# Moving the SBUF tiles of a two-layer encoder trunk to other start addresses

## The chip, the cores and the metric

The kernel runs on one core of a Trainium2 chip. The metric is device time in microseconds (us) of one execution. Engines are named as the profile names them: PE multiplies, PEld is PE's loading of the stationary operand, DVE (VectorE) and ACT (ScalarE) work element by element, SP issues the DMAs. All addresses below are bytes within one SBUF partition.

## The reference, cut to what matters

The input is 256 tokens of 1024 features. Two layers, each: half a SwiGLU step, a mixer step, half a SwiGLU step; every step is normalised, scaled and shifted by values that a condition vector `c` gives, and added back through a gate. Layer 0 mixes by pooling, layer 1 by differential attention. All in float32.

```python
for i in range(DEPTH):
    mod = (c_act @ mod_w[i] + mod_b[i])[:, None, :]
    sh0, sc0, g0, sh1, sc1, g1, sh2, sc2, g2 = jnp.split(mod, N_MOD, axis=-1)
    h = modulate(rms_norm(x, norm_g[i, 0]), sh0, sc0)
    x = x + 0.5 * g0 * swiglu(h, ffn_w_gu[i, 0], ffn_w_down[i, 0])
    h = modulate(rms_norm(x, norm_g[i, 1]), sh1, sc1)
    ...  # y: pool_mixer (i = 0) or diff_attention (i = 1)
    x = x + g1 * y
    h = modulate(rms_norm(x, norm_g[i, 2]), sh2, sc2)
    x = x + 0.5 * g2 * swiglu(h, ffn_w_gu[i, 1], ffn_w_down[i, 1])
return rms_norm(x, final_g)
```

## The kernel before, in words

Activations stay in SBUF, features on partitions, 256 tokens along the row. The weights come from HBM once, as 312 units of up to 128 x 1024 float32 (4096 bytes a row), in the order in which they are used. To keep float32 accuracy with the narrower matmul type fp32r, every operand is held as two parts. `split_unit` (lines 304 to 316) loads a unit into `raw`, lets ACT write `hi` (line 313) and DVE write `lo = raw - hi` (line 314). These live in three rings: `raw` with 5 buffers, `hi` and `lo` with 6 each. The activations have parts too: `hh`/`hl` (the normalised input), `ahl` (the inner activations; `ah`, `al` are its halves), `xh`/`xl` (the not yet normalised input).

A product of two split operands is three matmuls (`prod3`, lines 331 to 335): L333 multiplies the two high parts, L334 and L335 a high by a low part. In most of the program a 128 x 128 piece of the weights, from `hi` or `lo`, is the stationary operand (512 bytes of each partition's row are loaded) and 256 tokens of `hh`, `hl`, `ah` or `al` are the moving operand (1024 bytes of each row). In `v_unit` and in the pooling mixer it is the other way round: `hi` or `lo` moves and a piece of the activations is loaded. The first weights of a step use `xh`/`xl` instead (`mm_deferred`, L431 to L433), with the normalisation applied afterwards; there a moving row of `xh` is 258 columns wide, and the rows of `xh` lie 258 x 4 = 1032 bytes apart.

Beside this, DVE does the products of the condition vector with `mod_w` (line 272, one tile `u` of 128 x 1024 at a time, spread over the program as a background).

A scheduling layer places the instructions and inserts the waits. Where a tile lies is decided by the order in which the pools are opened and by the sizes of the tiles in them, each rounded up to 32 bytes. Before, small tiles stood among large ones: `eps1` (4 bytes, 32 with rounding) ahead of `xT`, the rows of `xh` with 8 odd bytes each, and `vecT`, `mod0`, `b1` and the other vectors between `cact` and the weights' rings.

Of the kernel before, what the change touches and what calls it, by code (L numbers as in the profile page):

```python
# [11 lines left out]
F32 = mybir.dt.float32  # L12
F32R = mybir.dt.float32r
# [3 lines left out]
AX = mybir.AxisListType  # L17

P = 128
D = 1024  # L20
KD = D // P
T = 256
NT = T // P
DFF = 2816
KF = DFF // P
EPS = 1e-6
# [36 lines left out]
def weight_units():  # L63

    def block(name, lead, r0, r1, c0, c1):
        return name, (*lead, slice(r0, r1), slice(c0, c1))

    def halves(name, lead, c0):
        yield block(name, lead, 0, 512, c0, c0 + UW)
        yield block(name, lead, 512, 1024, c0, c0 + UW)  # L70

    def ffn(i, s):
        first = 0
        if (i, s) == (0, 0):
            first = EARLY
            for k in range(KD):
                for n in range(2):
                    yield block("ffn_w_gu", (i, s), k * P, (k + 1) * P, n * DFF, n * DFF + EARLY * UW)
        for j in range(first, KF // 2):
            for n in range(2):  # L80
                yield from halves("ffn_w_gu", (i, s), n * DFF + j * UW)
        for dp in range(D // UW):
            for k0, k1 in DOWN_K:
                yield block("ffn_w_down", (i, s), k0 * P, k1 * P, dp * UW, (dp + 1) * UW)

# [5 lines left out]
    for tok in SCHED.split():  # L91
        n, u = tok[0], int(tok[1])
        if n in "qkv":
            yield from halves("diff_w_qkv", (), "qkv".index(n) * D + u * UW)
        elif n in "AB":
# [5 lines left out]
def unit_shape(ix):  # L101

    return (ix[-2].stop - ix[-2].start) // P, ix[-1].stop - ix[-1].start

# [8 lines left out]
def lay_out(inputs):  # L113
# [4 lines left out]
    head = np.concatenate([np.arange(16, 64), np.arange(0, 16), np.arange(64, P)])  # L118
    order = np.concatenate([h * P + head for h in range(2 * HEADS)] + [np.arange(2 * D, 3 * D)])
    w["diff_w_qkv"] = w["diff_w_qkv"][:, order]  # L120
    w["pool_w"] = w["pool_w"].reshape(D, UW)
    w["k_pool"] = consts["k_pool"]
# [20 lines left out]
def trunk(ctx: ExitStack, tc: tile.TileContext, x, c, mod_w, small, weights, diff_lambda, k_rope, out):  # L143
    nc = tc.nc
    V, S, PE = nc.vector, nc.scalar, nc.tensor

    cpool = ctx.enter_context(tc.tile_pool(name="cpool", bufs=1))
    rawp = ctx.enter_context(tc.tile_pool(name="rawp", bufs=RAW_BUFS))
    hip = ctx.enter_context(tc.tile_pool(name="hip", bufs=SPLIT_BUFS))
    lop = ctx.enter_context(tc.tile_pool(name="lop", bufs=SPLIT_BUFS))  # L150
    tmp = ctx.enter_context(tc.tile_pool(name="tmp", bufs=2))
    ps = ctx.enter_context(tc.tile_pool(name="ps", bufs=4, space=bass.MemoryType.PSUM))

    uid = [0]

    def nm(s):
        uid[0] += 1
        return f"{s}_{uid[0]}"

    def const(shape, name, dt=F32):  # L160
        return cpool.tile(shape, dt, tag=name, name=name)

    def psum():
        return ps.tile([P, 512], F32, tag="mm", name=nm("mm"), bufs=4)
# [4 lines left out]
    def psmall():  # L169
        return ps.tile([P, 512], F32, tag="st", name=nm("st"), bufs=2)  # L170
# [2 lines left out]
        return tmp.tile([P, n], F32, tag=tag, name=nm(tag), bufs=bufs)  # L173

    def tiny(n, dt=F32, tag="tiny", bufs=8):
        return tmp.tile([P, n], dt, tag=tag, name=nm(tag), bufs=bufs)

    def tinyw(n, dt=F32):
        return tiny(n, dt, "tinyw", 8)

    def tinyv(n, dt=F32):
        return tiny(n, dt, "tinyv", 6)
# [4 lines left out]
        return v.rearrange("p (k o) -> p k o", o=1)  # L187


    ident = const([P, P], "ident")  # L190
    make_identity(nc, ident)
    ones = const([P, P], "ones")
    V.memset(ones, 1.0)

    pt = psum()
    for _ in range(WARM):
        PE.matmul(pt[:, :P], ones, ones, start=True, stop=True)

    eps1 = const([P, 1], "eps1")
    V.memset(eps1, 1.0)  # L200

    xT = const([P, KD, T], "xT")
    xh = const([P, KD, T + 2], "xh", F32R)
    xl = const([P, KD, T], "xl", F32R)
    hh = const([P, KD, T], "hh", F32R)
    hl = const([P, KD, T], "hl", F32R)
# [3 lines left out]
    def warm(f, after):  # L210

        S.activation(tiny(1, tag="warm", bufs=1), after, f, scale=0.0, bias=eps1)


    cact = const([P, D], "cact")
    for half in range(2):
# [132 lines left out]
    def newton(y, y0, v, t):  # L349
        V.tensor_tensor(t, y0, y0, ALU.mult)  # L350
        V.scalar_tensor_tensor(t, t, -0.5, v, ALU.mult, ALU.mult)
        V.scalar_tensor_tensor(y, t, 1.5, y0, ALU.add, ALU.mult)
# [27 lines left out]
    def rstd_cols():  # L380

        pt = psmall()
        for q in range(NT):
            PE.matmul(pt[:, q:q + 1], acc[:, q * P:(q + 1) * P], ones[:, 0:1], start=True, stop=True)
        v = tiny(NT)
        V.tensor_scalar(v, pt[:, :NT], 1.0 / D, EPS, ALU.mult, ALU.add)
        y = tmp.tile([P, NT], F32, tag="rstdc", name=nm("rstdc"), bufs=2)
        y0 = tiny(NT)
        S.activation(y0, v, AF.Abs_reciprocal_sqrt)
        newton(y, y0, v, tiny(NT))  # L390
        return y
# [167 lines left out]
    def pool_mixer(nxt):  # L559
# [5 lines left out]
        S.activation(hh[:, :, 0:P], bb, AF.Copy)  # L565
        V.tensor_tensor(hl[:, :, 0:P], bb, hh[:, :, 0:P].bitcast(F32), ALU.subtract)
        rstd = rstd_cols()

        def group(pt, g, q, lh, ll):
# [358 lines left out]
```

## Time and profile before

| | us |
|---|---|
| median of 3 runs | 934.19 |
| lowest and highest of them | 933.71, 940.46 |
| the profiled execution | 942.75 |
| its span, first to last instruction | 940.9 |
| PE busy in the span | 911.2 (97%) |
| DVE busy | 743.6 (79%) |
| ACT busy | 505.4 (54%) |

The profiled execution is 8.6 us above the median. Matmuls overlap: each is shown as about 280 ns long, while the next one starts some 118 ns after it. What a matmul costs PE in a row of matmuls is therefore the distance from one start to the next, and not its own length; the timeline gives the starts to 10 ns, so that the distance is taken over many matmuls.

### The profile page before, as it was taken

The numbers are of one execution on the slowest core, as the hardware profiler recorded it, in microseconds if no ns is written. First come the engines' busy times: TensorE is split into PE (matmuls) and PEld (weight loads), VectorE is DVE, ScalarE is ACT, GpSimd is POOL, SyncE is SP. The second block draws the span as 40 slices with busy tenths as digits, with TensorE's granted clock in tenths as the row PEclk, the third lists the DMA queues.
The fourth block names the chain that finished last, engine by engine and source line by source line (L and its number), as shares of the span: only waits on it lengthen the run. The fifth ranks groups of instructions, "written<-read, shape, count | busy, mean of one in ns | idle before, by whom it ended". The sixth has DMA issues, their size and how long they took to land.

```text
span 940.9 us, 18753 instructions
## 1 busy us (share of the span) xinstructions
PE 911.2 (97%) x7532; PEld 897.5 (95%) x7532; DVE 743.6 (79%) x1211; ACT 505.4 (54%) x771; POOL 0.7 (0%) x6
## 2 busy tenths in 40 slices
PE   7899999899999999999999999999999999999997
PEld 7898889798999999999999999999999999999996
DVE  5868888789999777887988888888888897666451
ACT  5564435445665445455654454557777765444541
POOL 0000000000000000000000000000000000000000
PEclk9999999999999999999999999999999999999998
DMA  8988999888659887898599888855546548655531
GB/s 339 355 301 304 317 335 357 298 313 285 245 192 324 288 282 265 299 317 285 179 356 324 311 304 306 264 194 162 158 132 224 185 154 277 193 182 181 169 122 45
DMA packets 68727, 238.18 MB, mean 253 GB/s; under 512 B 7968, under 2 KB 9248, under 8 KB 68640
## 3 DMA queue, kind: packets, MB, share of 16 engines
q1 hardware_dynamic: 68496, 236.88, 73.8%
q8 instruction: 59, 0.97, 0.4%
q14 instruction: 28, 0.23, 0.1%
q10 hardware_dynamic: 144, 0.11, 0.0%
HBM read 234.86 MB, written 1.05 MB: 251 GB/s over the span
## 4 chain that ended last, share of the span: by engine, by line
PE 72%; DMA 12%; DVE 8%; ACT 4%; issue 3%; SPq 1%; DVEq 0%; ACTq 0%
PE mm L333 18%; PE mm L335 18%; PE mm L334 17%; DMA raw<-in_weights_dram 10%; DVE u L272 3%; DVE lo L314 3%; PE hd L335 3%; PE hd L333 3%; PE hd L334 3%; ACT hi L313 2%; PE mm L431 2%; PE mm L433 2%; PE mm L432 2%; PE hd L644 1%; DMA u<-in_mod_w_dram 1%
## 5 line engine op out<-in xcount | busy, mean ns | idle before, releaser
L313 ACT ACTIVATE hi<-raw 128x1024 fp32r<-128x1024 f32 (+1 forms) x312 | 318.6, 1025 | 339.2 <-PE mm L334 170.0
L314 DVE TENSOR_TENSOR lo<-raw,hi 128x1024 fp32r<-128x1024 f32 (+1 forms) x312 | 366.6, 1181 | 139.7 <-ACT hi L313 137.5
L335 PE MATMUL mm<-hh,lo 128*128 128x256 f32 x992 | 276.6, 281 | 4.4 <-DVE lo L314 4.4
L333 PE MATMUL mm<-hh,hi 128*128 128x256 f32 x992 | 277.7, 281 | 0.1
L334 PE MATMUL mm<-hl,hi 128*128 128x256 f32 x992 | 276.7, 280 | 0.0
L335 PE MATMUL mm<-ahl,lo 128*128 128x256 f32 x768 | 215.1, 280 | 2.2 <-DVE lo L314 2.2
L333 PE MATMUL mm<-ahl,hi 128*128 128x256 f32 x768 | 215.1, 280 | 1.8 <-ACT hi L313 1.8
L334 PE MATMUL mm<-ahl,hi 128*128 128x256 f32 x768 | 214.7, 280 | 0.0
L335 PEld LDWEIGHTS mm<-hh,lo 128*128 128x128 f32 x992 | 185.5, 188 | 6.6 <-DVE lo L314 6.0
L333 PEld LDWEIGHTS mm<-hh,hi 128*128 128x128 f32 x992 | 186.6, 188 | 1.3 <-ACT hh L420 0.4
L334 PEld LDWEIGHTS mm<-hl,hi 128*128 128x128 f32 x992 | 186.6, 188 | 0.0
L272 DVE SCALAR_TENSOR_TENSOR u<-u,cact 128x1024 f32<-128x1024 f32 x144 | 173.9, 1218 | 0.2 <-DMA u<-in_mod_w_dram 0.2
L335 PEld LDWEIGHTS mm<-ahl,lo 128*128 128x128 f32 x768 | 144.1, 188 | 3.4 <-DVE lo L314 3.4
L333 PEld LDWEIGHTS mm<-ahl,hi 128*128 128x128 f32 x768 | 144.2, 188 | 2.5 <-ACT hi L313 2.2
L334 PEld LDWEIGHTS mm<-ahl,hi 128*128 128x128 f32 x768 | 144.2, 188 | 0.0
L333 PE MATMUL hd<-hh,hi 128*128 128x256 f32 x288 | 81.2, 282 | 5.9 <-ACT hi L313 5.9
L335 PE MATMUL hd<-hh,lo 128*128 128x256 f32 x288 | 81.6, 283 | 3.9 <-DVE lo L314 3.9
L334 PE MATMUL hd<-hl,hi 128*128 128x256 f32 x288 | 80.7, 280 | 0.0
L333 PEld LDWEIGHTS hd<-hh,hi 128*128 128x128 f32 x288 | 54.3, 189 | 6.5 <-ACT hi L313 6.5
L335 PEld LDWEIGHTS hd<-hh,lo 128*128 128x128 f32 x288 | 54.3, 188 | 5.2 <-DVE lo L314 5.1
L432 PE MATMUL mm<-xl,hi 128*128 128x256 f32 x208 | 58.8, 285 | 0.0
L433 PE MATMUL mm<-xh,lo 128*128 128x258 f32 x208 | 58.3, 282 | 0.0
(199 smaller groups left out, 1034.7 us busy)
## 6 DMA issues: line engine op xcount, KB each, us to landing
raw<-in_weights_dram SPq DMA_DIRECT2D x264, 512.0 KB, 4.6
u<-in_mod_w_dram SPq DMA_DIRECT2D x144, 512.0 KB, 5.5
raw<-in_weights_dram SPq DMA_DIRECT2D x48, 384.0 KB, 5.0
xT<-in_x_dram SPq DMA_DIRECT2D x2, 512.0 KB, 5.0
out_dram<-u SPq DMA_DIRECT2D x4, 256.0 KB, 2.5
cact<-in_c_dram SPq DMA_DIRECT2D x1, 512.0 KB, 7.1
pk<-qk SPq DMA_DIRECT2D x16, 32.0 KB, 2.9
qk<-pk SPq DMA_DIRECT2D x16, 32.0 KB, 2.0
```

Source lines behind the costliest of these rows:

```text
L272: return V.scalar_tensor_tensor(raw, raw, 1.0, cact, ALU.mult, ALU.mult, accum_out=out)
L313: S.activation(hi[:, :w], raw[:, :w], AF.Copy)
L314: splits.append(V.tensor_tensor(lo[:, :w], raw[:, :w], hi[:, :w].bitcast(F32), ALU.subtract).ins)
L333: PE.matmul(o, lh, rh, start=start, stop=False, **kw)
L334: PE.matmul(o, lh, rl, start=False, stop=False, **kw)
L335: PE.matmul(o, ll, rh, start=False, stop=stop, **kw)
L431: PE.matmul(o[:, :T + 2], hi[:, kk, cs], xh[:, k, :], start=(k == 0), stop=False)
L432: PE.matmul(o[:, :T], hi[:, kk, cs], xl[:, k, :], start=False, stop=False)
L433: PE.matmul(o[:, :T + 2], lo[:, kk, cs], xh[:, k, :], start=False, stop=(k == KD - 1))
L644: PE.matmul(sc[c2][:, q * T:(q + 1) * T], l[pr, 0, qs], r[pr, 1, :], start=(n == 0), stop=(n == 2))
```

## The change

The change moves tiles in SBUF. Tiles whose row is not a multiple of 16 elements (64 bytes), and the small temporaries, go into a pool of their own behind everything else; the row of `xh` is widened to 272 columns, of which 258 are used; and one 64-byte tile `gap`, which is written once and never read, stands between the activations and the rings.

```diff
@@
 P = 128
+LINE = 16
@@
     cpool = ctx.enter_context(tc.tile_pool(name="cpool", bufs=1))
+    gap = ctx.enter_context(tc.tile_pool(name="gap", bufs=1))
     rawp = ctx.enter_context(tc.tile_pool(name="rawp", bufs=RAW_BUFS))
...
     tmp = ctx.enter_context(tc.tile_pool(name="tmp", bufs=2))
+    small_p = ctx.enter_context(tc.tile_pool(name="small_p", bufs=1))
@@
     def const(shape, name, dt=F32):
-        return cpool.tile(shape, dt, tag=name, name=name)
+        return (cpool if shape[-1] % LINE == 0 else small_p).tile(shape, dt, tag=name, name=name)
@@
     def tiny(n, dt=F32, tag="tiny", bufs=8):
-        return tmp.tile([P, n], dt, tag=tag, name=nm(tag), bufs=bufs)
+        return small_p.tile([P, n], dt, tag=tag, name=nm(tag), bufs=bufs)
@@
+    V.memset(gap.tile([P, LINE], F32, tag="gap", name="gap"), 0.0)
@@
-    xh = const([P, KD, T + 2], "xh", F32R)
+    xh = const([P, KD, T + LINE], "xh", F32R)[:, :, :T + 2]
@@
-        y = tmp.tile([P, NT], F32, tag="rstdc", name=nm("rstdc"), bufs=2)
+        y = tiny(NT, F32, "rstdc", 2)
```

On PE, ACT, SP and GpSimd the instructions, their order and their waits are the same in both programs; on DVE one MEMSET of 128 x 16 (`gap`) is added as the first instruction. All else that differs is the start addresses. Counted off from the sizes and the order of the tiles, they are (start of the row, modulo 256 and modulo 64):

```
tile                            before: mod 256, mod 64     after: mod 256, mod 64
xT                              160, 32                     128, 0
xh (row of each k)              160 + 8k, 32 + 8k           128 + 64k, 0
xl, hh, hl, ahl, cact           224, 32                     128, 0
raw, hi, lo (all buffers)       160, 32                     192, 0
u, t, qk, o, pk                 192, 0                      192, 0
ident, ones                     128, 0                      128, 0
acc                             128, 0                      128, 0
rstd, rope                      0, 0                        192, 0
```

All further steps inside a tile (from one k or one buffer to the next, from one 128-column piece to the next) are multiples of 512 bytes, so every matmul that reads a tile other than `xh` starts on the residue shown. The weights' parts start 64 bytes below the activations' residue before (160 against 224), and 64 bytes above it after (192 against 128).

## Rows read from the trace of the kernel before

**Rows 1.** The page: the span, each engine's busy time (share of the span, x instructions), and the chain of work that ended last, shared out by engine.
```profile
span 940.9 us, 18753 instructions
PE 911.2 (97%) x7532; PEld 897.5 (95%) x7532; DVE 743.6 (79%) x1211; ACT 505.4 (54%) x771; POOL 0.7 (0%) x6
...
PE 72%; DMA 12%; DVE 8%; ACT 4%; issue 3%; SPq 1%; DVEq 0%; ACTq 0%
```

**Rows 2.** Busy time in stretches of the program: from:to in us, then length, PE, PEld, DVE, ACT, POOL busy us (x instructions), granted TensorE clock (1.00 is its upper level, 2.4 GHz), share of the DMA engines, GB/s. 182 to 239 is the end of the first feed-forward step and the start of the pooling mixer; 239, 437 and 737 begin stretches with `xh`/`xl`; 625 to 737 is the attention.
```profile
47.00:182.00 135.00, 124.13 (x1008) 119.74 (x1009) 110.36 (x156) 65.15 (x81) 0.00 (x0) 1.00 0.90 319
182.00:239.00 57.00, 54.47 (x436) 54.07 (x435) 49.53 (x80) 27.68 (x40) 0.00 (x0) 0.94 0.83 289
239.00:279.00 40.00, 39.42 (x327) 38.86 (x327) 39.33 (x86) 28.19 (x50) 0.00 (x0) 1.00 0.70 243
279.00:437.00 158.00, 158.00 (x1343) 158.00 (x1343) 126.21 (x171) 76.70 (x96) 0.00 (x0) 1.00 0.87 294
437.00:469.00 32.00, 31.99 (x265) 31.52 (x264) 29.70 (x64) 20.07 (x32) 0.00 (x0) 1.00 0.59 184
469.00:625.00 156.00, 156.00 (x1326) 156.00 (x1326) 130.43 (x183) 78.19 (x98) 0.00 (x0) 1.00 0.87 301
625.00:737.00 112.00, 111.11 (x912) 106.00 (x911) 95.93 (x233) 82.42 (x199) 0.00 (x0) 1.00 0.56 175
737.00:774.00 37.00, 36.91 (x305) 36.41 (x304) 35.28 (x77) 27.37 (x47) 0.00 (x0) 1.00 0.47 153
774.00:924.00 150.00, 150.00 (x1276) 149.97 (x1274) 89.94 (x103) 69.65 (x85) 0.00 (x0) 1.00 0.56 180
```

**Rows 3.** Who waited for whom from 47 to 182 us: waiting engine and line, what it waited for: us in total, times, longest us.
```profile
ACT hi L313 <- DMA raw<-in_weights_dram: 40.3, 25, 5.0
...
PEld mm L335 <- DVE lo L314: 8.9, 13, 1.2
```

**Rows 4.** The same view from 279 to 437 us.
```profile
ACT hi L313 <- PE mm L334: 50.3, 34, 2.2
...
ACT hi L313 <- DMA raw<-in_weights_dram: 2.8, 1, 2.8
```

**Rows 5.** Timeline of PE (start us, length us), first and last of 102 matmuls without a gap in the second feed-forward step of layer 0.
```profile
299.91 0.28 PE L335 MATMUL mm<-hh,lo 128*128 128x256 f32 x1
...
311.81 0.28 PE L334 MATMUL hd<-hl,hi 128*128 128x256 f32 x1
```

**Rows 6.** The same view, first and last of 47 matmuls in the first feed-forward step.
```profile
144.02 0.28 PE L333 MATMUL hd<-hh,hi 128*128 128x256 f32 x1
...
149.24 0.28 PE L334 MATMUL mm<-hl,hi 128*128 128x256 f32 x1
```

**Rows 7.** The same view, two runs in which the weights' parts move (`v_unit`): first and last of 48 matmuls, then first and last of 31.
```profile
674.43 0.28 PE L333 MATMUL mm<-hi,hh 128*128 128x256 f32 x1
...
679.96 0.28 PE L335 MATMUL mm<-hi,hl 128*128 128x256 f32 x1
...
700.80 0.28 PE L335 MATMUL mm<-hi,hl 128*128 128x256 f32 x1
...
704.20 0.28 PE L335 MATMUL mm<-hi,hl 128*128 128x256 f32 x1
```

**Rows 8.** The same view, runs of alike matmuls merged (first start, time to the end of the last, xcount): eight transposes of 128 columns (moving `ident`, loaded `u`), and sixteen products of attention weights with values (moving operand two pieces of 512 bytes of `ahl`, loaded operand `ahl` too).
```profile
704.32 1.04 PE L675 MATMUL st<-ident,u 128*128 128x128 f32 x8
...
723.39 2.07 PE L694 MATMUL st<-ahl 128*128 128x256 f32 x16
```

**Rows 9.** The same view, the three matmuls of `mm_deferred` on k = 4 (the one row of `xh` that starts on a multiple of 64 before) and the first on k = 5.
```profile
269.47 0.28 PE L431 MATMUL hd<-xh,hi 128*128 128x258 f32 x1
...
269.83 0.28 PE L431 MATMUL hd<-xh,hi 128*128 128x258 f32 x1
```

**Rows 10.** Groups of DVE and ACT instructions by shape (line, engine, operation, out<-in, shapes, xcount | busy us, mean ns of one | idle before).
```profile
L314 DVE TENSOR_TENSOR lo<-raw,hi 128x1024 fp32r<-128x1024 f32 x264 | 321.2, 1222 | 131.8 <-ACT hi L313 129.9
L272 DVE SCALAR_TENSOR_TENSOR u<-u,cact 128x1024 f32<-128x1024 f32 x144 | 173.9, 1218 | 0.2 <-DMA u<-in_mod_w_dram 0.2
...
L822 DVE TENSOR_TENSOR qk<-xT,pk 128x1024 f32<-128x1024 f32 x1 | 1.2, 1218 | 0.0
```

**Rows 11.** The page's DMA issues (KB each, median us from issue to landing).
```profile
raw<-in_weights_dram SPq DMA_DIRECT2D x264, 512.0 KB, 4.6
u<-in_mod_w_dram SPq DMA_DIRECT2D x144, 512.0 KB, 5.5
```

**Rows 12.** Timeline of DVE from the span's start.
```profile
0.83 0.17 DVE L193 MEMSET ones<- 128x128 f32 x1 [0.83 <-PEq L916]
0.95 0.06 DVE L200 MEMSET eps<- 128x1 f32 x1
```

**Rows 13.** The chain that ended last, in order of time, near its start.
```profile
2.96 7.94 DMA u<-in_mod_w_dram
```

## The prediction, on record before the result

> **What bounds the kernel now.** I read the page first. PE is busy 97% of the span and carries 72% of the chain that ended last; DMA carries 12% of it [rows 1]. Whether a cheaper matmul shortens the program is a question of the stretch, so the table by stage comes next [rows 2]. Up to 182 us the weights' supply sets the pace: PE is busy 124.1 of 135 us, the DMA engines 90%, and ACT's split waits 40.3 us for arriving weights, after which PE waits for `lo` [rows 2, 3]. From 279 on it is the other way round. PE has no idle time in 279 to 437, 469 to 625 and 774 to 924, and the split waits for PE to give a ring buffer back (50.3 us against 2.8 for DMA) [rows 2, 4]. There the time is the number of matmuls times the distance from one start to the next, and nothing else.
>
> That distance is the number to look at. In the long stretches it is 11.90 us over 101 steps, 117.8 ns [rows 5]. With the same tiles on the same residues, another run goes at 5.22 us over 46 steps, 113.5 ns [rows 6]. Where the weights' parts move and lie 64 bytes below the loaded operand, which for the moving operand is the relation that the change gives to all matmuls, one run has 5.53 over 47, 117.7 ns, and another 3.40 over 30, 113.3 ns [rows 7]. So there are two levels, 4.4 ns apart, held for a whole run, at a granted clock of 1.00 (2.4 GHz) throughout. Neither is set by the shape alone. Eight transposes, whose moving operand starts at 128 and whose loaded operand at 192 modulo 256 (the residues after the change), take 1.04 us; with 0.27 for the last that is 0.77 over 7, 110 ns [rows 8]. They move 128 columns and not 256, so they do not prove what 256 will do, but 113.4 less one more step of 4.4 is 109, and the two agree within the timeline's rounding.
>
> **The change part by part.** No instruction but one moves, so everything hangs on what an instruction takes at its new addresses.
>
> (a) *Moving and loaded operands on multiples of 64, weights 64 above.* The rows of before have no 256-column matmul at these residues. Its spacing is bounded from below by the transposes and the step of the levels (109), from above by a level higher than today's, 117.8 + 4.4 = 122.2. Nothing excludes a loss: sixteen products whose moving and loaded operands start on the same residue go at (2.07 - 0.28) / 15 = 119 ns [rows 8]. I take 109: the transposes have the addresses, and the run of 113.5 shows that 117.8 is no floor.
>
> The gain is then 8.8 ns for each matmul in a stretch that PE bounds:
> - 279 to 437, 469 to 625, 774 to 924: 1343 + 1326 + 1276 = 3945 matmuls, 34.7 us, all on the path.
> - The three stretches with `xh`/`xl` hold 327 + 265 + 305 = 897 matmuls, 7.9 us if all got it. Here DVE is busy 39.3 of 40, 29.7 of 32 and 35.3 of 37 us, so it binds right after PE, and rows of 258 columns need not reach the level of 256. I take half, 4.0.
> - Attention, 912 matmuls, 8.0 us if all got it; part are of other shapes, PE runs in short pieces and idles 0.9 us. I take a third, 2.7.
> - 182 to 239, 436 matmuls, 3.8 us if all got it. The DMA engines are 83% busy and PE idles 2.5 us; I take nothing, and nothing before 182, where PE would only wait longer.
> - After 924 some 60 matmuls, 0.5 us.
>
> Sum 41.9 us, with all counts from the table by stage [rows 2].
>
> [...] In rows 5 and 6 all starts are multiples of 32. [...]
>
> (b) *Rows of `xh` 1088 bytes apart.* On k = 4, the only row that starts on a multiple of 64 today, three matmuls take 0.36 us, 120 ns each [rows 9]: no better than the rest. Aligning `xh` alone, against weights that are not, buys nothing visible, which is why half was taken above.
>
> (c) *DVE and ACT at new addresses.* DVE takes 1222 ns for 1024 columns with `raw` and `hi` at 160, 1218 with `u` at 192 and `cact` at 224, 1218 with `xT` at 160: the start does not show [rows 10]. Zero, within 4 ns a unit, and 312 of those are 1.2 us on an engine that has 20% to spare.
>
> (d) *DMA into `raw` at 192 instead of 160.* A unit lands in 4.6 us at 160; `u` is at 192 already and takes 5.5 with the same bytes, by its place in the queue [rows 11]. I take zero; were it 1% of the supply before 182, it would be 1.4 us either way.
>
> (e) *The MEMSET of `gap`.* It stands ahead of `ones` on DVE; its kin take 0.06 and 0.17 us [rows 12]. PE's warm-up matmuls wait for them, but the first weights' work waits until about 10.9 us for `u` [rows 13], so that covers it. Uncovered it would be 0.17 us.
>
> *What is late next.* With 109 ns, 279 to 437 moves its bytes in 146 us and needs 294 x 117.8 / 109 = 318 GB/s, and 469 to 625 needs 325; the stretch in which supply binds has 319 [rows 2]. At worst the second one is held to 156 x 301 / 319 = 147.2 us instead of 144.3: 2.9 us of the gain. DVE's 130.4 us fit into 144. This goes into the range.
>
> The profiled execution is 942.75, so it would come out at 900.9; subtracted from the median of 934.19 the same 42 us give 892.
>
> **The rivals.**
> - *One level instead of two.* The matmuls go to 113.4, the level that before shows in short runs, and stay there: 4.4 / 8.8 of the sum, 21 us, 913. For it: this is the only better spacing that 256 columns show, and the weights-move runs, with the relation of the change, never fall under it. Against it: those runs still start 32 bytes off a multiple of 64.
> - *The change does not do what it is laid out for.* The level is picked by how a run starts (both levels occur on one set of residues), long runs settle on 117.8 again, and the time is 934, give or take 9. For it: the slow run with the moved weights has the new relation and 117.7 all the same; k = 4 of `xh` gains nothing. [...]
> - *Slower.* Two streams that start on whole lines 64 bytes apart meet each time, where streams half a line off miss each other, and matmuls settle one level higher, 122.2 ns. At 4.4 more for the matmuls of the sum that is 21 us, 955. It decides from 119.8 ns on, where the loss passes 1%. For it: the 119 ns of the products on one common residue. Against it: the transposes with these very residues are the quickest of all.
>
> **How the numbers follow.** Two levels down 0.50 (from 882, which is nearly the whole 8.8 ns everywhere, 54.9 us, to 904, if the spacing is 111.5), one level 0.20 (908 to 918), no change 0.18 (925 to 943), slower 0.12. A measurement of this kernel can tell about 1%, 9 us, from no change. The likeliest is 892. A range from 882 to 936 holds nearly all of the first case, the second, and some two thirds of the third, together about 0.8. Faster by over 1%: 0.50 + 0.20 = 0.70; within 1% 0.18; slower 0.12.
>
> **What would show it.** In the timeline after, starts in the long stretches 109 ns apart, and the 1343 matmuls of 279 to 437 done in 146 us. The spacing in `v_unit` and pooling, which get the relation that the main matmuls have today, will tell the 64 bytes from the alignment: if alignment alone is the cause they fall too, if the relation is, they go to 117.8. The start up to 182 us, DVE's 1222 ns and the units' landing time should stay. I am wrong if the spacing stays at 117.8 or rises, or if it falls and PE then waits for `lo` after 279.

## The result and the profile after

The changed kernel takes 927.93 us (median of 20 runs, 919.33 to 940.43), the kernel before, run beside it, 938.52 (20 runs, 932.89 to 944.51). The ratio is 0.987, 95% interval 0.9843 to 0.9896; the ratios here and below leave out a kernel's runs over 1.5% above its fastest (four of the twenty here, four of the ten at +320, one of the twelve of the changed kernel further down), which may only be executions with slower stretches; the quotient of all medians is 0.9887. It is faster by 10.6 us, about 1.1%, where 42 us were forecast.

The profiled execution is 934.82 us. The page after, to be read against [rows 1], is hardly different:

```profile
span 933.0 us, 18754 instructions
PE 902.1 (97%) x7532; PEld 888.5 (95%) x7532; DVE 742.6 (80%) x1212; ACT 506.6 (54%) x771; POOL 0.7 (0%) x6
```

The table by stage gives the place (columns as in [rows 2]). The three lines of `prod3` are L339 to L341 now, each six lines below its place before.

```profile
47.00:182.00 135.00, 123.14 (x1007) 118.92 (x1008) 111.19 (x157) 66.31 (x82) 0.00 (x0) 0.99 0.90 323
182.00:239.00 57.00, 54.67 (x450) 54.48 (x450) 49.93 (x81) 28.08 (x40) 0.00 (x0) 0.93 0.81 283
239.00:279.00 40.00, 39.47 (x328) 38.90 (x327) 39.26 (x87) 28.27 (x49) 0.00 (x0) 1.00 0.69 244
279.00:437.00 158.00, 157.99 (x1341) 157.78 (x1341) 126.11 (x172) 77.25 (x96) 0.00 (x0) 1.00 0.86 296
...
469.00:625.00 156.00, 155.97 (x1370) 155.72 (x1370) 135.31 (x198) 81.51 (x104) 0.00 (x0) 1.00 0.89 308
...
774.00:924.00 150.00, 150.00 (x1277) 149.84 (x1277) 82.85 (x95) 66.25 (x82) 0.00 (x0) 1.00 0.52 167
```

Against [rows 2], 279 to 437 and 774 to 924 do the same number of matmuls in the same time as before (1341 against 1343, 1277 against 1276). Only 469 to 625 does clearly more, 1370 against 1326, and 182 to 239 adds 14.

Since a program that has run ahead has other matmuls in the same microseconds, the gain itself is read from marks. Both programs run the same 7532 matmuls in the same order; the marks are the first `mm_deferred` matmul of layer 1's first feed-forward step, of the attention, and of the last feed-forward step, first before, then after:

```profile
435.00 0.28 PE L431 MATMUL mm<-xh,hi 128*128 128x258 f32 x1
...
622.87 0.29 PE L431 MATMUL mm<-xh,hi 128*128 128x258 f32 x1
...
742.98 0.28 PE L431 MATMUL mm<-xh,hi 128*128 128x258 f32 x1
```
```profile
433.35 0.28 PE L437 MATMUL mm<-xh,hi 128*128 128x258 f32 x1
...
615.36 0.28 PE L437 MATMUL mm<-xh,hi 128*128 128x258 f32 x1
...
735.19 0.28 PE L437 MATMUL mm<-xh,hi 128*128 128x258 f32 x1
```

At the first mark 1.65 us have been gained, at the second 7.51, at the third 7.79. So 5.86 us come from the piece with the stretch of 469 to 625, and the attention gives 0.28. The first 1.65 come from 183 to 230 us, where some 398 matmuls follow one another without a gap; by their starts in the trace they stand 117.6 ns apart before and 113.4 after. Nearly all of the 7.9 us between the two profiled executions is in these two places.

The timeline says at which spacing (start us, length us). First and last of 107 matmuls without a gap in 279 to 437, then of 110 in 469 to 625:

```profile
299.68 0.28 PE L341 MATMUL mm<-hh,lo 128*128 128x256 f32 x1
...
312.16 0.28 PE L339 MATMUL hd<-hh,hi 128*128 128x256 f32 x1
...
483.78 0.28 PE L339 MATMUL mm<-hh,hi 128*128 128x256 f32 x1
...
496.13 0.28 PE L340 MATMUL hd<-hl,hi 128*128 128x256 f32 x1
```

12.48 us over 106 steps is 117.7 ns, as in [rows 5]; 12.35 over 109 is 113.3, as in [rows 6]. These are the two levels of before, and no stretch of 256 columns goes at 109. What has changed is how often the lower one is held. In the three long stretches (some 1,300 matmuls each without a gap) the means by starts are 117.8, 117.8, 117.8 before and 117.8, 113.4, 117.7 after. Of the runs of at least 12 matmuls between 20 and 182 us, 6 of 27 went at the lower level before and 18 of 25 after (counted by a mean under 117 ns; two of the 18 mix both levels and have 116.1). There supply sets the pace and nothing is gained: 47 to 182 has 1007 matmuls against 1008.

A long stretch keeps its level from its first few matmuls nearly to its end. Where the level changes, one step is longer, here beside a weight load that comes late. PE and PEld at the place, shortly ahead of 469, from which that stretch has 113.3:

```profile
464.12 0.28 PE L339 MATMUL mm<-hh,hi 128*128 128x256 f32 x1
464.24 0.28 PE L340 MATMUL mm<-hl,hi 128*128 128x256 f32 x1
464.35 0.28 PE L341 MATMUL mm<-hh,lo 128*128 128x256 f32 x1
464.47 0.28 PE L339 MATMUL mm<-hh,hi 128*128 128x256 f32 x1
464.59 0.30 PE L340 MATMUL mm<-hl,hi 128*128 128x256 f32 x1
464.73 0.28 PE L341 MATMUL mm<-hh,lo 128*128 128x256 f32 x1
...
465.31 0.28 PE L340 MATMUL mm<-hl,hi 128*128 128x256 f32 x1
...
465.65 0.28 PE L340 MATMUL mm<-hl,hi 128*128 128x256 f32 x1
```
```profile
464.36 0.19 PEld L339 LDWEIGHTS mm<-hh,hi 128*128 128x128 f32 x1
464.50 0.19 PEld L340 LDWEIGHTS mm<-hl,hi 128*128 128x128 f32 x1
```

Each load starts within 10 ns of the matmul beside which it runs (464.35 and 464.36), but the one at 464.50 starts 30 ns behind that of 464.47. Ahead of it the starts are 117.7 ns apart, one step of 140 follows, and behind it they are 113.3 apart up to the end of the stretch. The late load by itself doesn't turn the level over: in the kernel before the load of the same matmul comes late too, and 117.8 goes on.

```profile
466.09 0.28 PE L333 MATMUL mm<-hh,hi 128*128 128x256 f32 x1
...
466.11 0.19 PEld L334 LDWEIGHTS mm<-hl,hi 128*128 128x128 f32 x1
```

### The profile page after: what moved, and what is told of

It is laid out like the page before. It is cut to its first block, busy times and chain, and to the rows that moved or that the text cites. A ratio compares the mean times of both kernels' runs of the same rounds, so it can differ in the third digit from the quotient of the medians.

```text
span 933.0 us, 18754 instructions
## 1 busy us (share of the span) xinstructions
PE 902.1 (97%) x7532; PEld 888.5 (95%) x7532; DVE 742.6 (80%) x1212; ACT 506.6 (54%) x771; POOL 0.7 (0%) x6
## 4 chain that ended last, share of the span: by engine, by line
PE 73%; DMA 11%; DVE 8%; ACT 3%; issue 3%; SPq 1%; DVEq 0%; ACTq 0%
PE mm L339 18%; PE mm L341 18%; PE mm L340 18%; DMA raw<-in_weights_dram 9%; DVE u L278 3%; DVE lo L320 3%; PE hd L341 3%; PE hd L339 3%; PE hd L340 2%; PE mm L438 2%; PE mm L437 2%; PE mm L439 2%; ACT hi L319 2%; PE hd L650 1%; DMA u<-in_mod_w_dram 1%
## 5 line engine op out<-in xcount | busy, mean ns | idle before, releaser
L341 PE MATMUL mm<-hh,lo 128*128 128x256 f32 x992 | 276.4, 281 | 4.9 <-DVE lo L320 4.8
L339 PE MATMUL mm<-hh,hi 128*128 128x256 f32 x992 | 277.3, 281 | 0.0
L340 PE MATMUL mm<-hl,hi 128*128 128x256 f32 x992 | 276.6, 280 | 0.0
L341 PE MATMUL mm<-ahl,lo 128*128 128x256 f32 x768 | 215.1, 280 | 2.5 <-DVE lo L320 2.5
L339 PE MATMUL mm<-ahl,hi 128*128 128x256 f32 x768 | 215.2, 280 | 1.5 <-ACT hi L319 1.5
L340 PE MATMUL mm<-ahl,hi 128*128 128x256 f32 x768 | 214.7, 280 | 0.0
L341 PEld LDWEIGHTS mm<-hh,lo 128*128 128x128 f32 x992 | 187.7, 190 | 7.2 <-DVE lo L320 6.9
L339 PEld LDWEIGHTS mm<-hh,hi 128*128 128x128 f32 x992 | 186.9, 189 | 1.0 <-ACT hh L426 0.3
L340 PEld LDWEIGHTS mm<-hl,hi 128*128 128x128 f32 x992 | 187.2, 189 | 0.0
L341 PEld LDWEIGHTS mm<-ahl,lo 128*128 128x128 f32 x768 | 146.4, 191 | 3.4 <-DVE lo L320 3.3
L339 PEld LDWEIGHTS mm<-ahl,hi 128*128 128x128 f32 x768 | 145.0, 189 | 2.2 <-ACT hi L319 1.9
L340 PEld LDWEIGHTS mm<-ahl,hi 128*128 128x128 f32 x768 | 145.0, 189 | 0.0
L339 PE MATMUL hd<-hh,hi 128*128 128x256 f32 x288 | 81.3, 282 | 6.3 <-ACT hi L319 6.3
L341 PE MATMUL hd<-hh,lo 128*128 128x256 f32 x288 | 81.8, 284 | 3.5 <-DVE lo L320 3.5
L340 PE MATMUL hd<-hl,hi 128*128 128x256 f32 x288 | 80.8, 280 | 0.0
L339 PEld LDWEIGHTS hd<-hh,hi 128*128 128x128 f32 x288 | 54.6, 190 | 6.9 <-ACT hi L319 6.9
L341 PEld LDWEIGHTS hd<-hh,lo 128*128 128x128 f32 x288 | 55.0, 191 | 5.0 <-DVE lo L320 4.9
```

The source lines that it names most:

```text
L339: PE.matmul(o, lh, rh, start=start, stop=False, **kw)
L340: PE.matmul(o, lh, rl, start=False, stop=False, **kw)
L341: PE.matmul(o, ll, rh, start=False, stop=stop, **kw)
```

## The experiments

d is the start of the weights' parts less that of the activations, modulo 256: -64 before, +64 after. "Long" are the three long stretches' means, "early" the runs before 182 us, both by starts in one profiled execution.

### The relation with alignment, and without it

In the changed kernel, without the gap (d = 0):

```diff
-    gap = ctx.enter_context(tc.tile_pool(name="gap", bufs=1))
...
-    V.memset(gap.tile([P, LINE], F32, tag="gap", name="gap"), 0.0)
```

> The changed kernel without the 64-byte gap: everything still on multiples of 64, but the weights' parts now start on the same residue as the activations (128 and 128 modulo 256). If the start on a multiple of 64 is what helps, the short runs of matmuls sit at 113.4 ns as often as in the changed kernel (about 7 in 10) and the time stays near 928. If the 64 bytes between the two are what helps, most runs go back to 117.8 and the time to about 938. If neither matters and every run draws its level by chance, time and shares agree with those of the changed kernel and also with those of the kernel before within their scatter.

In the changed kernel, rings and gap opened ahead of the activations' pool (all aligned, d = -64 as before):

```diff
-    cpool = ctx.enter_context(tc.tile_pool(name="cpool", bufs=1))
-    gap = ctx.enter_context(tc.tile_pool(name="gap", bufs=1))
...
+    gap = ctx.enter_context(tc.tile_pool(name="gap", bufs=1))
+    cpool = ctx.enter_context(tc.tile_pool(name="cpool", bufs=1))
```

> The rings are allocated ahead of the activations: multiples of 64 everywhere, weights' parts 64 bytes below the activations modulo 256 (128 against 192), the relation of the kernel before. Alignment theory: as the changed kernel, about 928, most short runs at 113.4. Relation theory: as the kernel before, about 938, most short runs and all three long ones at 117.8. The moved-weights runs of attention and pooling then have the other relation and should go to 113.4.

In the changed kernel, a gap of 128 bytes (d = 128); in this run two one-column constants, `nlam` and `subs`, share one tile as well:

```diff
-    V.memset(gap.tile([P, LINE], F32, tag="gap", name="gap"), 0.0)
+    V.memset(gap.tile([P, 2 * LINE], F32, tag="gap", name="gap"), 0.0)
```

> The changed kernel with a gap of 128 bytes: multiples of 64, weights' parts half of 256 away from the activations (0 against 128). Alignment theory: about 928. Relation theory: open, between 919 (all three long stretches at 113.4) and 938 (all at 117.8). A level near 109 in any of the four layouts would revive the predicted spacing: time near 895.

In the kernel before, a gap ahead of the rings and nothing else, so that all stays 32 past a multiple of 64. 128 bytes give d = +64; the next three runs have 24, 40 and 96 elements in place of 32 (d = +32, +96, and +320, which is 64 modulo 256):

```diff
+    gap = ctx.enter_context(tc.tile_pool(name="gap", bufs=1))
...
+    V.memset(gap.tile([P, 32], F32, tag="gap", name="gap"), 0.0)
```

> The kernel before with 128 bytes put between activations and rings: activations still at 224 modulo 256, 32 off a multiple of 64, weights' parts at 32 modulo 256, which is 64 above. Relation theory: as the changed kernel, about 928, most short runs at 113.4. Alignment theory: as the kernel before, about 938, about 1 short run in 8 at 113.4.

> The kernel before with 96 bytes between activations and rings: weights' parts 32 bytes above the activations (0 against 224 modulo 256). The theory by now: the spacing in a run is set by where the weights start against the activations, 120.0 ns at 0 bytes, 113.4 or 117.8 at 64. If it goes by pieces of 64 bytes, the half step lies between its neighbours: spacing between 113.4 and 120.0, time between 928 and 951, about 940. If only whole multiples of 64 matter, it equals one of the two neighbours. A spacing under 113 would be a new, lower level, time below 915.

> The same with 160 bytes: weights' parts 96 above (64 against 224). Its neighbours are 64 (113.4 or 117.8 ns, 928 to 930) and 128 (118.7 or 120.0 ns, 947). By pieces of 64: between them, about 938. A better place than 64 would show a spacing of 113.4 in all long stretches, about 919, or less.

> The same with 384 bytes: weights' parts 64 + 256 = 320 above. If the relation counts modulo 256, as the change takes it, the result is that of 64 above: about 930, short runs of matmuls at 113.4 in more than half of all cases. If it counts modulo 512, it is another relation and need not be: any spacing from 113.4 to 120.

Measured:

```
start (mod 64), d     us (runs)    ratio to before         long                  early at 113.4
aligned, 0            951.0 (6)    1.012  [1.009, 1.015]   120.0  120.0  120.0   0 of 24
aligned, -64          939.2 (12)   1.000  [0.997, 1.002]   117.8  117.8  117.7   4 of 27
aligned, 128          947.0 (10)   1.008  [1.006, 1.011]   118.7  118.7  120.0   0 of 25
32 off, +64           930.3 (6)    0.990  [0.987, 0.994]   117.8  117.8  113.3   19 of 24
32 off, +32           943.6 (10)   1.002  [0.999, 1.005]   118.4  118.4  118.3   0 of 25
32 off, +96           941.8 (10)   1.001  [0.998, 1.004]   117.4  118.7  118.6   0 of 28
32 off, +320          932.6 (10)   0.985  [0.981, 0.990]   117.8  113.5  117.8   20 of 27
```

The stage 279 to 437 of d = 0, of aligned -64 and of unaligned +64 in turn (columns as in [rows 2]):

```profile
279.00:437.00 158.00, 158.00 (x1319) 158.00 (x1318) 123.28 (x167) 74.75 (x91) 0.00 (x0) 1.00 0.86 292
```
```profile
279.00:437.00 158.00, 157.97 (x1341) 157.74 (x1339) 126.01 (x172) 77.40 (x96) 0.00 (x0) 1.00 0.87 297
```
```profile
279.00:437.00 158.00, 158.00 (x1340) 157.77 (x1339) 125.89 (x172) 77.61 (x96) 0.00 (x0) 1.00 0.87 297
```

The two bottom rows show the level that both kernels have there; 158 us over 1319 is 119.8 ns, a level above. Aligned with the old relation is the kernel before, and the new relation without alignment is the changed kernel within the intervals. So where weights are loaded and activations move, the relation is the cause of the more frequent 113.4, and the multiples of 64 are worth nothing. One single relation, +64 (and +320), gives 113.4 often; on the others tried, except -64, it never appeared. No expectation had foreseen that a relation can be worse than the old one: d = 0 and d = 128 lie above the 938 that was their highest.

Where the weights move (`v_unit` and the mixer, beside `hh` and `hl`) the sign is turned round, and there it decides little. Of seven such runs of at least 12 matmuls, four went at the lower level in the kernel before and four in the aligned -64 (both +64 there), three in the changed kernel and one in the unaligned +64 (both -64 there). That these runs go to 113.4 in the aligned -64 came true for four of seven, as many as in the kernel before.

### Whose weights, and how much of the matmul

The changed kernel again, for a second profile. Then one ring alone moved:

> The changed kernel once more, for a second profile. Theory: each run of matmuls draws 113.4 or 117.8 at its start and keeps it, so the long stretches that were at 113.4 and 117.8 in the first profile need not be the same ones here; the time follows their number, about 5.8 us for each long stretch. Rival: the level is a fixed property of place and layout, and the same stretch is at 113.4 again, run for run.

```diff
+    lop = ctx.enter_context(tc.tile_pool(name="lop", bufs=SPLIT_BUFS))
     gap = ctx.enter_context(tc.tile_pool(name="gap", bufs=1))
...
-    lop = ctx.enter_context(tc.tile_pool(name="lop", bufs=SPLIT_BUFS))
```

> The changed kernel with one ring, that of the rounded lower parts (lo), moved 64 bytes down, ahead of the gap: lo starts as the activations do modulo 256, the other rings (raw, hi) 64 bytes above them as in the changed kernel. Theory (what counts is the tile that is being loaded for the next matmul against the rows that move at that moment): the matmuls beside which a lo tile is loaded stand about 120 ns apart, as all of them do with every ring at the same residue (119.99), and those beside which a hi tile is loaded 113.4 to 118; a run's mean lies between, near 115.5 to 119. Rival (what counts is a matmul's own weights against its own rows): the matmuls that use a lo tile as weights show the 120 ns, those with a hi tile as weights 113.4 to 118, with the same mean. Rival (not the pair but one spacing for the whole program): all passes alike. The time by the first two: 935 to 948 us.

The repeat took 929.5 us: long 117.8, 113.5, 117.8, early 23 of 28. The same long stretch is at 113.4 again, so that the repeat alone leaves the rival open; a third profile of the changed kernel, further down, has 113.3, 113.3, 117.8, and that rules out a level fixed by place. With `lo` at d = 0 one execution took 938.1 (before beside it 935.8): long 117.8, 117.8, 117.8, early 0 of 27. There, within a product, all three passes had the same step:

```profile
300.03 0.28 PE L341 MATMUL mm<-hh,lo 128*128 128x256 f32 x1
300.15 0.28 PE L339 MATMUL mm<-hh,hi 128*128 128x256 f32 x1
300.26 0.28 PE L340 MATMUL mm<-hl,hi 128*128 128x256 f32 x1
300.38 0.28 PE L341 MATMUL mm<-hh,lo 128*128 128x256 f32 x1
```

In these three stretches both theories of a cost by pass fall, since no pass is at 120. But the price showed in seven early runs of 47 or 48 matmuls, and in the 398 without a gap from 181 to 229. Ten of them:

```profile
199.70 0.28 PE L341 MATMUL mm<-ahl,lo 128*128 128x256 f32 x1
...
200.80 0.28 PE L341 MATMUL mm<-ahl,lo 128*128 128x256 f32 x1
```

1.10 us over 9 steps is 122 ns. Up to 225 the step behind L340, during which `lo` is loaded for L341, has a mean of 127.5, the one behind L339 121.7 and the one behind L341 117.5. That is the pass of the first theory, at a higher price than its 120; the rival, by which L341 itself would pay, falls. So this layout too has two states, and one third of the loads at d = 0 was enough to keep 113.4 away from both: the spacing belongs to a train of loads and matmuls, not to a pair of tiles alone.

The map of offsets: blocks of 40 extra matmuls in one program, slices of `hh` as weights.

```diff
+    def block(d, cols=T, wide=P, n=40):
+        fixed, moved = hh.rearrange(F), hl.rearrange(F)
+        c = d // 4
+        for k in range(n):
+            w = T * (k % 6) + c
+            m = T * (k % 7)
+            PE.matmul(spare[0][:wide, :cols], fixed[:, w:w + wide], moved[:, m:m + cols], start=(k == 0), stop=(k == n - 1))
...
```

> The changed kernel with extra work only, some 2,900 matmuls that nobody reads, ahead of the first gate product of the first of the three later feed-forward steps: blocks of 40 matmuls of 256 moving columns (hl) on 128 by 128 weights (slices of hh), the slices starting 0, 16, ... 240 bytes past the moving rows modulo 256; once upwards, once downwards, once with one matmul of 96 columns ahead of each block, once with one of 64 columns; then blocks with 64 columns of weights and blocks with 128 moving columns, at 0, 64, 128 and 192. Theory (the load of the next weights takes its reads from the same memory as the moving rows, and their relation modulo 256 sets by how much): 120 at 0, 118.4 at 32, 113.4 or 117.8 at 64, 117.4 or 118.7 at 96, 118.7 at 128, 117.8 or 113.4 at 192, and nowhere under 113; with half the columns of weights the spacing falls to 109 to 113, since there is half as much to load. Rival (there is an offset at which load and rows don't meet, as the prediction had it for 64): one or more of the untried offsets at 108 to 110. Rival (the offsets mattered by the place of the tiles, not by their relation): one or two levels over the whole map, without order. The time: some 340 us above the changed kernel.

Spacing in ns by d, blocks taken upwards, downwards, each behind 96 columns, each behind 64:

```
d      0     16    32    48    64    80    96    112   128   144   160   176   192   208   224   240
up   120.0 118.3 118.4 117.8 113.3 118.9 118.6 120.2 120.0 118.4 120.1 118.0 117.8 116.7 116.7 119.9
down 120.0 118.2 118.3 117.8 113.3 119.9 118.5 119.8 118.6 116.7 120.2 118.0 117.8 116.7 116.8 119.9
96   120.0 118.5 118.3 117.8 117.8 119.8 117.4 120.2 118.8 120.0 120.1 118.2 117.8 116.7 116.5 120.1
64   120.0 118.5 118.3 117.8 117.8 118.7 118.5 120.2 118.9 120.0 119.9 118.0 117.8 116.6 117.8 117.3
```

Some of its blocks (alike matmuls merged: first start, time to the end of the last, xcount): d = 64 upwards, d = 0 downwards, d = 64 behind 64 columns, then 64 columns of weights at d = 0 and at 128, and last a block with 128 moving columns.

```profile
294.62 4.47 PE L492 MATMUL st<-hl,hh 128*128 128x256 f32 x38
...
422.43 4.48 PE L492 MATMUL st<-hl,hh 128*128 128x256 f32 x36
...
524.56 4.17 PE L492 MATMUL st<-hl,hh 128*128 128x256 f32 x34
...
582.37 4.36 PE L492 MATMUL st<-hl,hh 128*64 128x256 f32 x37
...
591.33 4.48 PE L492 MATMUL st<-hl,hh 128*64 128x256 f32 x37
...
604.82 4.63 PE L492 MATMUL st<-hl,hh 128*128 128x128 f32 x40
```

Less 0.28 for the last and over the steps between, the first five give 113.2, 120.0, 117.9, 113.3, 116.7. Nowhere is there a 109. At 208 all four passes have 116.6 to 116.7, under the 117.8 of the old relation whatever stood ahead. At half the weights, where 109 to 113 was expected, the least is 113.3. With half of the weights d = 0 falls from 120.0 to 113.3 (64 and 192 have 113.3 too, 128 has 116.7). With whole loads d alone moves the spacing between 113.3 and 120, the moving rows being the same. Together these say that the load stretches the matmul; that half a load also means half the output rows was not separated. The blocks with 128 moving columns stood at 111.6 to 111.7 on all four offsets: there the relation doesn't matter, and half the columns to move save under 2 ns of 113.3, so that something other than the moving of columns sets their spacing. That this is the load is likely and not shown. Nor is it shown how a load stretches a matmul from 113.3 to 120.0 at d = 0, by its reads or otherwise.

### What picks the level

One extra matmul (`hh` times `hh`, n columns, no reader) ahead of every gate and up product of the three later feed-forward steps, n = 8, 32, 64, 96, 128, 192, 256 in turn; first in the changed kernel, later in the one before.

```diff
...
+            PE.matmul(spare[0][:, :n], hh[:, 0, 0:P], hh[:, 0, :n], start=True, stop=True)
...
```

> The changed kernel with extra work only: ahead of every gate and every up product of the three later feed-forward steps one small extra matmul of 8, 32, 64, 96, 128, 192 or 256 columns in turn, with no reader. In the changed kernel each of the three long stretches keeps one of two spacings (113.4 or 117.8 ns) almost from its first matmul to its last, and what moved it over was a weight load that came late. Theory (the spacing is a phase between loads and matmuls, which any break in the rhythm draws again): the spacing changes between products within a stretch, after some sizes more often to 113.4 than after others, and the mean over the three stretches lies between the two, 115 to 117 ns. Rival (the spacing of a stretch is set by its place, its tiles or its neighbours' work): each long stretch stays at 117.8, 113.4 and 117.8 as in the changed kernel, with the extra matmuls as the only breaks. The extra matmuls cost their own time, by the 117.8 ns of 256 columns some 10 to 118 ns each.

> The kernel before with the same extra matmuls of 8, 32, 64, 96, 128, 192 and 256 columns in turn ahead of the later gate and up products as in the map on the changed kernel. With the weights' parts 64 bytes below, 96 columns always left 117.8 where above they always left 113.4. Theory (the two layouts mirror each other: the same two spacings, the phase of a start turned round): other sizes leave 113.4 here, above all 128 or 256, which left 117.8 in the layout above; some of the stretches at 113.3, the mean at 115 to 117 ns. Rival (below, 117.8 is where every start goes, and 113.4 is a rare accident of the early runs): 117.8 behind all sizes.

In the changed kernel (933.2 us with the 54 extra matmuls) the level alternated within the long stretches, and the same size had the same outcome each time: from the fourth product of a step on, 113.3 behind 8, 64, 96 and 192 columns, 117.8 behind 32, 128 and 256. Two of them in the timeline, 128 columns and, 5.7 us later, 192:

```profile
288.46 0.28 PE L340 MATMUL hd<-hh,hi 128*128 128x256 f32 x1
...
288.80 0.22 PE L487 MATMUL st<-hh 128*128 128x128 f32 x1
288.86 0.33 PE L340 MATMUL mm<-hh,hi 128*128 128x256 f32 x1
...
294.21 0.28 PE L340 MATMUL mm<-hh,hi 128*128 128x256 f32 x1
...
294.57 0.25 PE L487 MATMUL st<-hh 128*128 128x192 f32 x1
294.65 0.31 PE L340 MATMUL mm<-hh,hi 128*128 128x256 f32 x1
```

Three steps take 0.34 us ahead of the first (113.3 by the starts over a product) and 0.36 ahead of the second (117.8). 8, 32 and 64 take PE the same 30 ns, and 8, 64 and 192 always met 117.8 there while 32, 128 and 256 always met 113.3; so a disturbance may simply turn the level over. In the first of the three steps 32 columns, ahead of the second product, met 117.8 and left 113.3, which speaks for that. Only 96 met both and left 113.3 each time. Nor is that a rule for all places: in the map of offsets 96 columns ahead of d = 64 left 117.8. A late load draws the level anew in the same way without deciding it: the one shown ahead of 469 is 20 ns late in the kernel before and 117.8 stays, 26 in the changed kernel and 117.8 turns to 113.3, 59 in its repeat and 113.3 stays, 53 in the unaligned +64 and 113.3 turns to 117.8. In the kernel before, with the same 54 (944.4 us), every size left 117.8; 113.4 came up in one place only, behind three other gaps at 272 to 283 us.

Then 96 columns alone, nine times, ahead of the third, fourth and eleventh product of each step, in both kernels:

```diff
+NUDGES = [96 if n in (2, 3, 10) else 0 for n in range(18)]
...
```

> The changed kernel with extra work only: nine extra matmuls of 96 columns that nobody reads, three in each of the three later feed-forward steps (ahead of the third, the fourth and the eleventh of its 18 gate and up products). In the map of sizes 96 columns left 113.3 ns behind them each time, whether the products before had stood at 117.8 or at 113.3. Theory (the spacing is a phase that a disturbance draws again, always in the same way for one size and one phase before it): all three long stretches at 113.4 ns, where the changed kernel has 117.8, 113.4 and 117.8; two stretches of some 1,300 matmuls gain 4.4 ns each, 11.5 us, less nine times 0.117 us for the extra work: 10.4 us, 917 to 919 us against 928. Rival (another limit, the weights' arrival above all, takes over as soon as the three stretches run at 113.4): the stretches at 113.4 but with waits in them, 922 to 928 us. Rival (the phase is lost again within a stretch): two of the three or fewer at 113.4, 922 to 929 us.

> The kernel before, its layout untouched (parts 64 bytes below the activations modulo 256, 32 past a multiple of 64), with the same nine extra matmuls of 96 columns and no reader. Its three long stretches stood at 117.8 ns, and six of its 27 early runs at 113.4. Theory (both relations, 64 below and 64 above, have the same two spacings, and the layout alone decides how often a run's start lands on the shorter one): if 96 columns draw the shorter spacing here too, all three stretches stand at 113.4, 3 x 5.9 = 17.7 us less 1.1 for the extra work, 921 to 923 us against 938.5; the layout of the change is then needed for nothing that a small extra matmul doesn't give. Rival (with the parts 64 bytes below, the phase after 96 columns is the longer one, since the start of a run differs in the two layouts): 117.8 in all three and 939 to 940 us. Rival (below, the shorter spacing doesn't last in long runs): stretches that start at 113.4 and go over to 117.8, 925 to 938 us.

The changed kernel with the nine: 925.64 us (6 runs, 920.86 to 928.66), ratio to before 0.9873 [0.9836, 0.991]; all three long stretches at 113.3 to 113.4. Three of the nine met 117.8 and left 113.3 (the first up to the next break, a few steps on), six met 113.3 and kept it. The kernel before with the nine: 939.54 (12 runs), 1.0013 [0.9991, 1.0035]; 117.8 behind all nine. The stages of the former (774 to 910, since the program is shorter):

```profile
279.00:437.00 158.00, 157.97 (x1385) 157.72 (x1384) 128.58 (x182) 81.46 (x101) 0.00 (x0) 1.00 0.89 303
469.00:625.00 156.00, 155.97 (x1367) 155.72 (x1366) 132.50 (x197) 78.91 (x100) 0.00 (x0) 1.00 0.87 296
774.00:910.00 136.00, 136.00 (x1201) 135.84 (x1200) 76.63 (x90) 61.98 (x78) 0.00 (x0) 1.00 0.52 159
```

PE has no wait in them: supply at 303 GB/s holds, so the rival of a new limit falls. The time of 917 to 919 was missed all the same; 925.6 lies where the two rivals had it, though the mechanism of neither is there. To see what it is worth, both on one chip:

> The changed kernel itself once more, as the partner of the next run on the same chip. Its long stretches draw 113.4 or 117.8 ns anew in each execution: by the two profiles so far one of three on the shorter one, so 927 to 930 us, with single executions from 919 to 940.

> The changed kernel with the nine extra matmuls of 96 columns, timed beside the changed kernel on the same chip. Theory (the three long stretches always stand at 113.4 ns, and in the changed kernel one or two of three): 5 to 11 us under the changed kernel, 918 to 925 us, and a smaller spread, since executions with slow stretches are gone. Rival (in executions without a profile the changed kernel's stretches are at 113.4 more often than the two profiles show, so that the extra matmuls mend little): 0 to 4 us under it, as the medians of the earlier runs have it (925.6 against 927.9).

The changed kernel: 929.36 (12 runs, 926.41 to 940.89), 0.991 [0.9882, 0.9939]; its profile (926.4 us) had two of the three long stretches at 113.4. With the nine: 923.12 (6 runs, 920.92 to 928.39), 0.9849 [0.9814, 0.9884], all three at 113.4. On this chip it is 6.2 us faster by the medians and less spread; over both chips its twelve runs have a median of 924.3. It has the lowest median here, though the two intervals against before overlap by a hair.

## Why the prediction was wrong

**The bound** was read right: in the long stretches the time is matmuls times spacing, and the other engines' work and the supply did not get in the way even at 113.4.

**Step (a) failed: the value 109.** It came from eight transposes of 128 columns on the new residues [rows 8], with "two levels less one more step" as the bridge. Transposes show 110 on other addresses too. The timeline has six transposes of `xT` at the end, with the loaded operand 32 above the moving one in the kernel before, and on the same residue after:

```profile
923.39 0.82 PE L896 MATMUL mm<-ident,xT 128*128 128x128 f32 x6
```
```profile
915.74 0.82 PE L902 MATMUL mm<-ident,xT 128*128 128x128 f32 x6
```

The first row is of the kernel before, the second of after; (0.82 - 0.27) / 5 is 110 ns in both. The first was there to be read, and would have shown that the low number was the transposes' own. For 256 columns, with a new load for every matmul, nothing under 113.3 was found at any of the 16 offsets tried.

**The second failure of (a) is the share.** 8.8 ns were counted for all 3,945 matmuls. The gain is 4.4 ns, and only for the stretches that happen to start on 113.4: one, one and two of three in the three profiles of the changed kernel. At 4.4 ns x 1,330 = 5.9 us each, 4/3 stretches give 7.9; with the 1.7 of the first mark and the 0.3 of the attention in the first of these profiles it is 9.9 us, against 10.6 measured. The sum is an estimate from three executions; the levels in the others are not known. That 927.93 lies within the stated range, 882 to 936, is due to the rivals that the range took in, and not to the step.

**The other terms.** The `xh` stretches gained nothing (328 matmuls against 327 in 239 to 279) where 4.0 were taken; of the rows of `xh`, which start at 128 + 64k, only one in four has the relation +64, which may be the reason and was not tested. The attention gave 0.3 for 2.7, and 182 to 239 1.7 for 0: it holds the 398 matmuls without a gap. DVE, the units' landing and the MEMSET of `gap` (0.07 us) were right: `lo` takes 1221 ns against 1222, `raw` lands in 4.6 us [rows 10 to 12].

**The rivals.** "One level" had the right size, 113.4, and "picked by how a run starts" the right reason why it isn't everywhere; each was given its own world, but the two hold together, and the time lies between their 913 and 934. "Slower" named a higher level, and one exists on another offset: streams that start on the same residue go at 120.0. That streams meet on lines, as it had it, no run shows. "No change" was right for alignment alone: the aligned -64 takes the time of the kernel before (ratio 1.000).

**The test that was named** (`v_unit`, with today's relation: falls or stays at 117.8) could not decide. After the change one run went at 1.42 us over 12 steps, 118 within the timeline's rounding, and another at 4.99 over 44, 113.4:

```profile
655.91 0.28 PE L341 MATMUL mm<-hi,hl 128*128 128x256 f32 x1
...
657.33 0.28 PE L341 MATMUL mm<-hi,hl 128*128 128x256 f32 x1
...
667.08 0.28 PE L339 MATMUL mm<-hi,hh 128*128 128x256 f32 x1
...
672.07 0.28 PE L341 MATMUL mm<-hi,hl 128*128 128x256 f32 x1
```

Both levels again, as in [rows 7]: three runs of seven at the lower one, where it was four of seven. [Rows 5] to [rows 7] already showed two levels on one set of residues, which said that residues alone do not set the spacing; the prediction used them as a ladder to go down instead.

Open stays what happens inside PE: why +64 starts so often on 113.4 and -64 so seldom. Open stays too why the nine extra matmuls gain 11.8 and 16.0 us by the medians, against the kernel before beside them, where 3 x 5.9 + 1.7 - 1.1 = 18 us were to be had. The two profiled executions, the only ones whose levels are known, took 920.9 and 922.6 us, 22 and 20 less than the profiled one before. Executions differ in more than the spacing: after a wait for DVE (2.2 us before, 2.3 after), PE works for a time at a granted clock of 0.5, so that the clock from 232 to 239 us is 0.52 in the mean before and 0.62 after, and 1.00 at d = 0, where PE doesn't wait there.

## What to carry to other kernels

Where matmuls follow one another without a gap, read their spacing from start to start in several stretches; if it has two values on the same tiles (113.3 and 117.8 here), look for what starts or disturbs a run before crediting an address. A better spacing must be taken from the same shape: a neighbour of another width shows its own floor (here 110 for transposes of 128 columns, 113.3 for 256). Where loaded and moving operands come from tiles whose order is free, a map of their offset modulo 256 costs one program with short blocks, and the worst choice of those timed (the same residue) is 1.2% slower here than the old one.

## What the runs showed that was not expected

A spacing is a state of the whole train: it survives 1,300 matmuls, and one break of some tens of ns can draw it anew. One ring in three on the same residue kept three long trains at 117.8 without any pass at 120, and a fourth at 122 with one pass in three at 127.5. And the same extra matmul of 96 columns, which costs about 117 ns (46 for itself, and 185 instead of 114 for the next step), led to 113.3 nine times of nine in each of two profiles with the weights above the activations, and to 117.8 nine of nine with them below.
